# The middle group of a down projection takes its row blocks backwards, and the sums of the block at each turn stay in SBUF

## The chip, the cores and the metric

One core of one Trainium2 chip runs one layer of a streaming encoder in float32. The metric is the device time of one execution in microseconds (us). The engines are TensorE (PE, with PEld for its weight loads), VectorE (DVE), ScalarE (ACT), GpSimd (POOL) and SyncE (SP); here SP issues nearly all DMAs.

## The reference

A layer has two branches (retention and a gated linear recurrence), merged, projected and added to the residual. Behind that stands a gated MLP, and its last matrix product is the one that the change is about:

```python
h = rms_norm(x, norm2_w[l])
up = h @ ffn_w_up[l]                       # 1024 x 1024 by 1024 x 6144
gate, val = jnp.split(up, [D_FF], axis=-1)
gate = causal_depthwise_conv(gate, ffn_conv_w[l], ffn_conv_b[l])
x = x + (jax.nn.gelu(gate) * val) @ ffn_w_down[l]   # 1024 x 3072 by 3072 x 1024
return rms_norm(x, norm_f_w)
```

There are 1024 positions, D_MODEL is 1024 and D_FF 3072.

## The kernel before

**Products.** A float32 operand is split into a high part and a low part in fp32r (`split`, L595 to L600: a cast on ACT at L598, a subtraction on DVE at L599), and a product of two operands is three matmuls (`PASSES`). A job multiplies a 256 x 1024 piece by a 1024 x 1024 operand. It does so by Strassen and Winograd's scheme (`mm_fast`, L827): seven products (`PRODS`: A11, S1, S2, A12, S3, A22, S4) of 4 x 3 = 12 matmuls in place of eight, so 84 matmuls make one job. The operand of the right side comes in seven sets of four tiles (B11, T1, T2, B21, T3, T4, B22), each tile as a high and a low part, 56 buffers in all.

**The down projection.** The 3072 rows of `ffn_w_down` are three groups of 1024, `g` = 0, 1, 2; each group has an operand `dop[g]` of its own. The 1024 rows of the output are four pairs of row blocks, `t` = 0 to 3: rows 128 t to 128 t + 127 (m = 0) and 512 higher (m = 1). With two column halves `c` a job (g, t) has four output tiles [128, 512]. `djobs` (L2125) runs the groups one after the other, and t = 0, 1, 2, 3 in each. The sums over the groups live in DRAM, in `x1_d`, which holds the residual stream: a job of any group loads its four tiles (`from_x1`, L2022 to L2027, issued at L2025 by SP), adds its product (L872 and L878 in `total`, or L2035 in `emit_down`), and in groups 0 and 1 stores them (L2039, SP). In group 2 the sum goes on to the final norm (`square`, `final`), with nothing written to `x1_d`.

Within a job the tiles are emitted in this order: (m, c) = (0, 0) after A12, (1, 1) after S3, (1, 0) after A22 and (0, 1) after S4. `ask` (L624) starts the loads one or two products ahead of that, in the program's order.

**The operand's builder.** `down_op` (L1958) loads 28 tiles of `w_dn` (L1962) or of prepared sums of them in `td_d` (L1969), and splits them. After the second job of a group, `down_post` (L2116) puts the builder of the next group's operand in a list; `build` (L741) lets it go on after each product, as long as the buffer pool has room:

```python
while builders and budget > 0 and len(U) >= state["reserve"] and U.free() >= SPARE:
```

The reserve is 12 (`TIGHT`) from then on, and `SPARE` is 8. The last job of a group (`last`) gives the operand's buffers back, eight after each product, so the next operand takes the places of the old one while that is used for the last time.

**Buffers.** The pool `u` has 81 buffers of [128, 512] float32 (`NU`). `get` takes the one that was given back first, `put` gives one back. Each buffer is a place in SBUF with a name of its own, so a get makes the instructions of the new owner wait for those of the old one.

**Order.** The program is built twice. From the first build `Plan.order` (L496) works out an order of the instructions of every queue (PE, DVE, ACT, POOL, SP): the draft with the least time in its own replays, out of some 150 drafts with offsets drawn at random. The second build is tied to that order. So the place of an instruction in its queue is the planner's; what may overtake what is limited by data and by the buffers.

In the profile `x1_d` is named x_d, and a PSUM bank of `mm_fast` is g.

Of the kernel before, what the change touches and what calls it, by code (L numbers as in the profile page):

```python
# [93 lines left out]
class Units:  # L94
# [18 lines left out]
    def get(self, dt=F32):  # L113
        _, _, i = heapq.heappop(self.q)
        self.count += 1
        t = self.pool.tile(self.shape, dt, tag=f"{self.name}{i}", name=f"{self.name}{i}_{self.count}")
        self.at[id(t)] = (i, t)
        return t

    def put(self, *tiles, late=LATE):  # L120
        for t in tiles:
            self.count += 1
            heapq.heappush(self.q, (self.now[0] + late, self.count, self.at.pop(id(t))[0]))
# [430 lines left out]
def tile_trunk_layer(ctx, tc, x, xt, front, positions, params, consts, normf, w_in, w_v, w_ro, w_lo,  # L554
# [983 lines left out]
    def from_sg_t1(n):  # L1538
        def fetch(m, h):
            t = get()  # L1540
            SY.dma_start(t, t1_d[2 * n + m, :, TH * h:TH * h + TH])
            return from_sg(1, n)(m, h), t
        return fetch
# [274 lines left out]
    for n in range(4):  # L1818
        ojobs.append(Job(pair_src(w_lo, n), u, emit_lru_o(n), fast=True, last=n == 3, mate=n in (0, 2),
                         fetch=from_sg_t1(n)))  # L1820
# [15 lines left out]
    def from_x(t):  # L1836
        def fetch(m, c):
            acc = get()
            SY.dma_start(acc, x[x_row(t, m, c)])
            return acc  # L1840
        return fetch
# [78 lines left out]
    def out_start():  # L1920
# [4 lines left out]
                 pre=((0, 0), (0, 1), (1, 1)), fetch=from_x(t), mate=t == 0, prods=FIRST if t < 2 else PRODS,  # L1925
# [32 lines left out]
    def down_op(g):  # L1958
        def fetch(n, j):
            t = get()  # L1960
            kh, c = int(n[1]) - 1, int(n[2]) - 1
            SY.dma_start(t, w_dn[8 * g + 4 * kh + j, :, TH * c:TH * c + TH])  # L1962
            return t

        def either(n, j):
            if n[0] == "B":
                return fetch(n, j)
            t = get()
            SY.dma_start(t, td_d[g, int(n[1]) - 1, j])  # L1969
            return t  # L1970

        yield from operand(dop[g], either, False, ("B11", "T1", "T2", "B21", "T3", "T4", "B22"))
# [45 lines left out]
    def x1_at(t, m, c):  # L2018
        r0 = 512 * m + 128 * t
        return x1_d[r0:r0 + 128, TH * c:TH * c + TH]  # L2020

    def from_x1(t):  # L2022
        def fetch(m, c):
            acc = get()
            SY.dma_start(acc, x1_at(t, m, c))  # L2025
            return acc
        return fetch  # L2027

    def emit_down(g, t, fast):
        def emit(m, c, src, unit):  # L2030
            if fast and unit is not None:
                acc = unit
            else:
                acc = djobs[4 * g + t].take(m, c)
                V.tensor_add(acc, src, acc)  # L2035
                if unit is not None:
                    put(unit)
            if g < 2:
                ST.dma_start(x1_at(t, m, c), acc)  # L2039
                put(acc)  # L2040
                return
            fin[m, c] = acc
            square(m, c)
            if (m, 1 - c) in fin:
                final(t, m, c)
        return emit

    def square(m, c):

        o, acc = get(), fin[m, c]  # L2050
        V.tensor_mul(o, acc, nf[c])
        j = psa.get()
        S.activation(j, acc, AF.Square, scale=1.0 / 32.0, accum_out=nst[:, c, 2 + m:3 + m])
        psa.put(j)
        put(acc)
        fin[m, c] = o
        if (m, 1 - c) not in fin:
            V.tensor_scalar(nst[:, c, 2 + m:3 + m], nst[:, c, 2 + m:3 + m], EPS, None, ALU.add)
        else:
            V.tensor_add(nst[:, 2, 2 + m:3 + m], nst[:, 0, 2 + m:3 + m], nst[:, 1, 2 + m:3 + m])  # L2060
# [29 lines left out]
    def final(t, m, c):  # L2090
        v, r = (nst[:, i, 2 + m:3 + m] for i in (2, 3))
        G.tensor_tensor(r, v, half[:, 0:1], ALU.pow)
        r0 = 512 * m + 128 * t
        def scaled(c):
            o = fin.pop((m, c))
            if (m, c) == (0, 1) or t == 3:
                ins = V.tensor_scalar(o, o, r, None, ALU.mult)
            else:
                ins = S.activation(o, o, AF.Copy, scale=r)
            (SY if c else nc.scalar).dma_start(out[r0:r0 + 128, TH * c:TH * c + TH], o)  # L2100
            put(o)
            return ins

        scaled(0)
        if t == 3:
            fin["rest"] = lambda: scaled(1)
        else:
            scaled(1)

    def norm_weights():  # L2110
        for c in range(2):
            t = get()
            SY.dma_start(t, normf[:, TH * c:TH * c + TH].to_broadcast((P, TH)))
            nf.append(t)

    def down_post(g, t):  # L2116
        def fn():
            if t == 1 and g < 2:
                state["reserve"] = TIGHT
                builders.append(down_op(g + 1))  # L2120
            if g == 1 and t == 3:
                norm_weights()
        return fn

    djobs = [Job(lambda m, kh, t=t, g=g: ff_d[g, 4 * m + t, kh].rearrange("p k c -> p (k c)"), dop[g],  # L2125
                 emit_down(g, t, True), down_post(g, t), fast=True, last=t == 3,
                 prods=ENDING if (g, t) == (2, 3) else PRODS,
                 halves=(slice(0, TH // 2), slice(TH // 2, TH)) if (g, t) == (2, 3) else (),
                 pre=((0, 0), (0, 1), (1, 1)), fetch=from_x1(t),
                 ready=lambda m, kh, g=g: state["ff"] >= 8 * g + 4 * kh + 4)  # L2130
             for g in range(3) for t in range(4)]
    queue.extend(ups + djobs)
    run(wjobs)
    run(ups)
# [66 lines left out]
```

## Time and profile before

| | us |
|---|---|
| median of 3 runs | 1565.41 |
| lowest, highest | 1564.99, 1566.33 |
| the profiled execution | 1564.81 |
| its span, first to last instruction | 1563.0 |
| granted clock of TensorE, mean | 0.999 |

The profile is of one execution. Its busy times are by engine; PE's matmuls are pipelined. A group of instructions is one line, engine, operation and tile; "waits" are the idle stretches of an engine just before an instruction, put down to what ended them. A DMA's duration on SP is that of its issue; the time to landing stands apart.

### The profile page before, as it was taken

How to read it: one execution, taken by the hardware profiler on the slowest of the kernel's cores; microseconds unless marked ns; L12 is line 12 of the kernel's file. 1: busy time of each engine (PE TensorE's matmuls, PEld its weight loads, DVE VectorE, ACT ScalarE, POOL GpSimd, SP SyncE). 2: the span in 40 equal slices, each digit the busy share in tenths (PEclk: the TensorE clock that was granted, in tenths of full speed). 3: DMA queues.
4: the chain of work that ended last, by engine and by line, in shares of the span. 5: the costliest groups of instructions: out<-in, count | busy, mean ns of one | idle time of the engine just before them, and what ended most of it. 6: DMA issues, size and time to landing. Idle time of an engine off the chain costs nothing.

```text
span 1563.0 us, 21782 instructions
## 1 busy us (share of the span) xinstructions
PE 1555.2 (99%) x7081; PEld 1289.0 (82%) x7081; DVE 1356.7 (87%) x2454; ACT 971.2 (62%) x1733; POOL 64.5 (4%) x81
## 2 busy tenths in 40 slices
PE   9999999999999999999999999999999999999998
PEld 7888888888888888888888888888888888888887
DVE  8999989999999988999998898777777778887885
ACT  8557967777678787855556665545545447463653
POOL 0001001000000000000000001000000000000000
PEclk9999999999999999999999999999999999999999
DMA  9344334455354336775995246444444476787752
GB/s 325 118 144 129 122 122 137 132 186 185 103 187 142 117 126 200 257 270 168 323 309 183 94 121 222 139 138 135 140 143 140 144 235 207 243 272 249 262 189 80
DMA packets 158577, 279.04 MB, mean 179 GB/s; under 512 B 17144, under 2 KB 30848, under 8 KB 158464
## 3 DMA queue, kind: packets, MB, share of 16 engines
q1 hardware_dynamic: 152800, 261.86, 51.4%
q0 software_dynamic: 4224, 13.64, 2.7%
q10 hardware_dynamic: 1440, 2.17, 0.4%
q8 instruction: 55, 0.90, 0.2%
q14 instruction: 58, 0.48, 0.1%
HBM read 192.65 MB, written 83.89 MB: 177 GB/s over the span
## 4 chain that ended last, share of the span: by engine, by line
PE 96%; ACT 2%; DMA 1%; issue 0%; DVE 0%; POOLq 0%; POOL 0%; SPq 0%; ACTq 0%
PE g L849 85%; PE g L1616 5%; PE a L1259 3%; PE a L1387 1%; DMA u<-td_d 1%; PE a L1401 1%; PE a L1390 1%; PE a L1893 0%; PE a L1377 0%; PE a L1460 0%; ACT w L598 0%; ACT u L598 0%; PE a L1335 0%; DMA cst<-front 0%; ACT L1215 0%
## 5 line engine op out<-in xcount | busy, mean ns | idle before, releaser
L849 PE MATMUL g<-u,w 128*128 128x512 f32 x6060 | 1409.2, 390 | 0.5 <-ACT u L901 0.5
L849 PEld LDWEIGHTS g<-u,w 128*128 128x128 f32 x6060 | 1128.2, 188 | 228.9 <-ACT u L901 1.7
L598 ACT CAST w<-w 128x512 fp32r<-128x512 f32 x519 | 318.8, 621 | 317.1 <-PE g L849 233.5
L599 DVE TENSOR_TENSOR w<-w,w 128x512 fp32r<-128x512 f32 x519 | 353.1, 686 | 81.0 <-ACT w L598 78.0
L598 ACT CAST u<-u 128x512 fp32r<-128x512 f32 x245 | 146.7, 619 | 59.1 <-PE g L849 7.5
L599 DVE TENSOR_TENSOR u<-u,u 128x512 fp32r<-128x512 f32 x245 | 161.9, 686 | 6.3 <-ACT u L598 2.4
L901 ACT COPY u<-g 128x512 f32<-128x512 f32 x148 | 86.2, 582 | 60.3 <-PE g L849 57.4
L878 DVE TENSOR_TENSOR u<-g,u 128x512 f32<-128x512 f32 x146 | 100.3, 688 | 21.3 <-PE g L849 17.2
L1945 DVE SCALAR_TENSOR_TENSOR u<-u,par,u 128x511 f32<-128x511 f32 (+1 forms) x96 | 71.7, 748 | 12.8 <-ACT u L1942 12.2
L1616 PE MATMUL g<-w,u 128*128 128x512 f32 x252 | 59.0, 390 | 0.0
L1616 PEld LDWEIGHTS g<-w,u 128*128 128x128 f32 x252 | 47.1, 188 | 10.3 <-ACT g L1678 0.4
L1950 POOL DMA_DIRECT2D ff_d<-u x48 | 36.1, 753 | 447.7 <-DVE u L1949 437.3
L684 DVE TENSOR_TENSOR w<-w,w 128x512 f32<-128x512 f32 x72 | 49.4, 686 | 2.3 <-DMA w<-mix_d 1.0
L898 ACT COPY g<-g 128x512 f32<-128x512 f32 x70 | 40.5, 578 | 16.4 <-PE g L849 16.4
L1259 PE MATMUL a<-u,u 128*128 128x512 f32 x192 | 50.2, 390 | 0.1
L687 DVE TENSOR_TENSOR w<-w,w 128x512 f32<-128x512 f32 x72 | 49.4, 686 | 0.6
L693 DVE TENSOR_TENSOR w<-w,w 128x512 f32<-128x512 f32 x72 | 49.3, 685 | 0.5 <-DMA w<-mix_d 0.4
L690 DVE TENSOR_TENSOR w<-w,w 128x512 f32<-128x512 f32 x72 | 49.4, 686 | 0.2
L1942 ACT ACTIVATE u<-u,par 128x512 f32<-128x512 f32 x48 | 39.2, 817 | 8.6 <-DVE u L878 6.9
L1259 PEld LDWEIGHTS a<-u,u 128*128 128x128 f32 x192 | 35.9, 188 | 8.0 <-ACT u L598 0.5
L872 DVE TENSOR_TENSOR u<-u,u 128x512 f32<-128x512 f32 x34 | 23.2, 688 | 20.5 <-ACT u L901 20.4
L1206 ACT COPY u<-g 128x512 f32<-128x512 f32 x56 | 32.5, 581 | 8.8 <-PE g L849 8.8
(222 smaller groups left out, 1218.2 us busy)
## 6 DMA issues: line engine op xcount, KB each, us to landing
w<-w_in SPq DMA_DIRECT2D x96, 256.0 KB, 2.7
w<-w_up SPq DMA_DIRECT2D x96, 256.0 KB, 2.7
u<-w_dn SPq DMA_DIRECT2D x84, 256.0 KB, 3.2
u<-x_d SPq DMA_DIRECT2D x52, 256.0 KB, 4.8
x_d<-u SPq DMA_DIRECT2D x48, 256.0 KB, 3.4
ff_d<-u POOLq DMA_DIRECT2D x48, 256.0 KB, 3.1
td_d<-u SPq DMA_DIRECT2D x48, 256.0 KB, 3.1
u<-td_d SPq DMA_DIRECT2D x48, 256.0 KB, 4.4
```

The costliest lines, as they stand in the source:

```text
L598: S.copy(hi, src)
L599: V.tensor_sub(lo, src, hi.bitcast(F32))
L684: V.tensor_add(s, r["A21"], r["A22"])
L687: V.tensor_sub(s, s, r["A11"])
L690: V.tensor_sub(s, r["A12"], s)
L693: V.tensor_sub(src, r["A21"], r["A11"])
L849: PE.matmul(bank[:, s], w[a][:, c], need(op, (SETS[nm], j))[b][:, s], start=first and n == 0, stop=n == 11, skip_group_check=True)
L878: V.tensor_add(u, bank, u)
L901: S.copy(u, bank)
L1259: PE.matmul(ps, wg[g][a][:, cs], xs[k][b], start=q == 0, stop=q == 5)
L1616: PE.matmul(bank, o[p][:, c], w[q], start=first and j == n == 0, stop=j == 3 and n == 2, skip_group_check=True)
L1945: V.scalar_tensor_tensor(c[:, s:], src[:, :TH - s], w, c[:, s:], ALU.mult, ALU.add)
```

## The change

The list `SNAKE` gives the order of the 12 jobs: group 0 takes t = 0, 1, 2, 3, group 1 takes 3, 2, 1, 0, and group 2 again 0, 1, 2, 3. So the last job of a group and the first one of the next work on the same row blocks: (0, 3) and (1, 3), (1, 0) and (2, 0). At these two turns the four output tiles aren't stored to `x1_d`: `emit_down` puts them in a dictionary `turn`, and the next job's fetch takes them from there in place of a new buffer and a load. What depended on t = 1 or t = 3 (the start of the next operand's builder, the load of the final norm's weights, and `last`) now goes by the place in the group.

```diff
+    SNAKE = [(g, t) for g in range(3) for t in ((3, 2, 1, 0) if g == 1 else (0, 1, 2, 3))]
+    turn = {}
+
-    def from_x1(t):
+    def from_x1(g, t):
         def fetch(m, c):
+            if g and SNAKE.index((g, t)) == 4 * g:
+                return turn.pop((m, c))
             acc = get()
             SY.dma_start(acc, x1_at(t, m, c))
             return acc
...
-                acc = djobs[4 * g + t].take(m, c)
+                acc = djobs[SNAKE.index((g, t))].take(m, c)
                 V.tensor_add(acc, src, acc)
                 if unit is not None:
                     put(unit)
+            if g < 2 and SNAKE.index((g, t)) == 4 * g + 3:
+                turn[m, c] = acc
+                return
             if g < 2:
                 ST.dma_start(x1_at(t, m, c), acc)
                 put(acc)
...
     def down_post(g, t):
         def fn():
-            if t == 1 and g < 2:
+            i = SNAKE.index((g, t)) - 4 * g
+            if i == 1 and g < 2:
                 state["reserve"] = TIGHT
                 builders.append(down_op(g + 1))
-            if g == 1 and t == 3:
+            if g == 1 and i == 3:
                 norm_weights()
         return fn
...
-                 emit_down(g, t, True), down_post(g, t), fast=True, last=t == 3,
+                 emit_down(g, t, True), down_post(g, t), fast=True, last=SNAKE.index((g, t)) % 4 == 3,
...
-                 pre=((0, 0), (0, 1), (1, 1)), fetch=from_x1(t),
+                 pre=((0, 0), (0, 1), (1, 1)), fetch=from_x1(g, t),
...
-             for g in range(3) for t in range(4)]
+             for g, t in SNAKE]
```

## The prediction

> **What bounds the kernel now.** I read the page first (busy shares and the costliest groups), then the waits of the matmul engine, then its timeline over the down projection, and last its pace in stretches with much and with little DMA traffic.
>
> ```profile
> span 1563.0 us, 21782 instructions
> PE 1555.2 (99%) x7081; PEld 1289.0 (82%) x7081; DVE 1356.7 (87%) x2454; ACT 971.2 (62%) x1733; POOL 64.5 (4%) x81
> ```
>
> PE is busy for 1555.2 of 1563.0 us, so 7.8 us of the span are not PE. The waits of PE over the whole span are two rows, and the second is the whole of those in the down projection:
>
> ```profile
> PE g L1651 <- DVE st L1825: 1.0, 1, 1.0
> PE g L849 <- ACT u L901: 0.5, 2, 0.3
> ```
>
> The timeline of PE from 1320 us on, and the first entry and the end of the chain of work that ended last:
>
> ```profile
> 1319.79 79.95 PE L849 MATMUL g<-u,w 128*128 128x512 f32 x352
> 1399.98 76.45 PE L849 MATMUL g<-u,w 128*128 128x512 f32 x336 [0.24 <-ACT u L901]
> 1476.72 80.23 PE L849 MATMUL g<-u,w 128*128 128x512 f32 x364 [0.29 <-ACT u L901]
> 5.20 2.68 PE g L1668 x10
> ```
>
> The down projection is 12 jobs of 7 products of 12 matmuls, so a group of four jobs is 336 matmuls: the middle piece, 76.45 us. PE stops for 0.24 us and for 0.29 us, one group apart. From a stop on, two products of the old group are left (A22 and S4, 24 matmuls by 76.45 / 336 = 0.2275 us, 5.5 us), so the turns between the groups lie near 1405.4 and 1482.2 us. The rest of PE's idle time is the start (first matmul at 5.20 us) and the end (the last matmul ends at 1476.72 + 80.23 = 1556.95, 6.05 us before the span does). The change touches neither: its first edit is an addition in the job ahead of the first turn, and the last job keeps its rows and its place.
>
> So the most that the change can save is 0.53 us of PE's waits, unless PE's own pace depends on the transfers. That is the next thing to look at (PE's stretches, with the DMA share and GB/s at the end of the row):
>
> ```profile
> 1388.20:1407.30 19.10, 18.86 (x83) 15.29 (x83) 17.80 (x30) 14.83 (x27) 0.00 (x0) 1.00 0.97 327
> 1407.30:1426.30 19.00, 19.00 (x85) 15.73 (x85) 15.19 (x25) 7.53 (x14) 0.00 (x0) 1.00 0.98 357
> 1521.70:1540.70 19.00, 19.00 (x85) 15.73 (x84) 13.06 (x25) 9.71 (x20) 1.52 (x2) 1.00 0.21 70
> 1540.70:1563.00 22.30, 16.25 (x84) 13.74 (x82) 10.61 (x24) 7.78 (x21) 1.76 (x3) 0.95 0.26 94
> ```
>
> The first two stretches hold the first turn, with the DMA engines full; the third is quiet. PE begins 85 matmuls in 19.00 us at a DMA share of 0.98 and 85 in 19.00 us at 0.21, with the granted clock at 1.00 in both. Its pace doesn't depend on the traffic.
>
> A rule of the Trainium skill speaks against reading 99% as a bound (Perfetto Trace Analysis, Identifying the Most-Contended Engine): matmul busy time says little of the distance to the peak, since matmuls are pipelined, and weight-load busy time is the better sign. By it the 82% on PEld would leave room that fewer transfers might free; the two equal stretches, with the same PEld 15.73, say that they would not.
>
> **The change part by part.**
>
> *Transfers removed.* At each of the two turns the four sums of one row block are neither stored (L2039) nor read back (L2025): 8 stores and 8 loads of 256 KB, 16 x 0.262 = 4.2 MB.
>
> ```profile
> DMA packets 158577, 279.04 MB, mean 179 GB/s; under 512 B 17144, under 2 KB 30848, under 8 KB 158464
> L2025 SPq DMA_DIRECT2D u<-x_d x48: 319/320/1409, 1261.0 to 1527.1; - x48
> DMA to landing us min/median/max: 2.5/5.1/6.5
> L2039 SPq DMA_DIRECT2D x_d<-u x32: 319/320/396, 1339.9 to 1488.4; - x32
> DMA to landing us min/median/max: 2.0/3.6/6.4
> ```
>
> Laid end to end they would be 8 x 5.1 + 8 x 3.6 = 69.6 us, and 16 x 0.32 = 5.1 us of SP's issue time. On the path stands none of it but what lies behind the two stops. These come from a chain that the waits of the other engines show:
>
> ```profile
> ACT u L598 <- DMA u<-td_d: 2.3, 3, 1.0
> ACT u L598 <- DMA u<-w_dn: 1.4, 1, 1.4
> ACT w L598 <- DMA w<-ff_d: 3.2, 1, 3.2
> ACT u L901 <- DMA x_d<-u: 2.3, 1, 2.3
> ...
> 1393.27 5.47 DMA u<-td_d
> 1398.74 0.02 issue
> 1398.76 0.02 ACTq L598
> 1398.78 0.04 issue
> 1398.82 0.62 ACT u L598
> 1399.44 0.49 ACT u L901
> ...
> 1466.26 5.88 DMA u<-td_d
> ```
>
> The next group's operand (28 tiles) is loaded and split in the last job of the old group. One of its loads lands after 5.47 us; ACT, which takes its instructions in order, holds the cast (L598) for it, the PSUM copy behind it (L901) comes late, and PE waits for that copy. In the same 1388 to 1407 us the DMA share is 0.97. Of the 16 removed transfers, few fall into the 5.5 us before each stop (SP's queue in the timeline):
>
> ```profile
> 1392.30 0.38 SPq L2025 DMA_DIRECT2D u<-x_d  x1
> ...
> 1394.92 0.38 SPq L2025 DMA_DIRECT2D u<-x_d  x1
> ...
> 1396.99 0.40 SPq L2039 DMA_DIRECT2D x_d<-u  x1
> ```
>
> The store at 1396.99 is the first kept sum's; of the x_d loads from 1392.30 to 1394.92, three in all, the trace doesn't tell whose they are. So the loads of the operand come sooner by somewhere between nothing and 256 KB at 327 GB/s, 0.8 us, for each transfer gone. One is enough for either stop. Bounds of this term: 0 and -0.53 us. I take half, **-0.27 us**, since this trace doesn't show whether the transfers gone are ahead of the load that is late.
>
> *Buffers held.* Four [128, 512] buffers of the pool `u` (81) stay taken from the emission in one job to the addition in the next: 84 matmuls by 0.2275, 19.1 us. Before, each was put back, and taken again one or two products ahead of its use. What this can delay is the builder of the next operand, which stops when the pool has fewer than 12 free (`reserve`, L743) or fewer than 8 that were freed long enough ago (`SPARE`). Followed through the allocations of the program before: from the first kept sum to the end of that operand, the builder is called with 24 to 33 buffers in the pool, 17 to 24 of them old enough. Four fewer leave at least 20 and 13, above 12 and 8. So the builder issues the same tiles at the same products. What does change is which buffer each get receives: one freed up to four releases later. Lower bound 0. Upper bound: the releases come in eights at the end of a product, so a load that needs such a buffer waits at most one product more, 12 x 0.2275 = 2.73 us a turn, 5.5 us in all, if no slack takes it up. Value: **0**, by the row nearest to it, the loads of td_d that already come late: ACT waits 2.3 us for them and PE only 0.5.
>
> *Rows backwards.* Group 1 reads its ff_d blocks in the order 3, 2, 1, 0; as many loads of the same size (L650). The nearest store and load of one row block of x1 move from four jobs apart to three (block 2 at the first turn, block 1 at the second): 3 x 19.1 = 57 us. A load can't go out before the store has landed; 57 less the longest store and the longest load, 6.4 and 6.5, leaves 44 us in which to issue it. Cost 0; that room is the cover, and a load that came late would hold L2035 or L872 on DVE and the splits (L599) queued behind.
>
> *Additions.* All stay: the kept tile is what L2035 or L872 adds to. In the job after a turn that addition waits for one of the job before on its own engine (DVE), 19 us earlier, in place of a DMA. DVE holds nothing behind it. Cost 0.
>
> *A new plan.* `Plan.order` writes the order of every queue from a search over the whole program (150 drafts with random offsets and landing times). Sixteen DMAs fewer give it other random numbers, so order moves everywhere, in stages that the change doesn't touch too. The trace of before can't show what the new draw costs. Lower bound: PE waits 1.5 us in all, so at best -1.0 us beyond the term above, and that 1.0 is at the start, where there is little to reorder: I take the lower end as -0.3. Upper bound by the nearest rows: the four waits of ACT for DMAs quoted above, 2.3 + 1.4 + 3.2 + 2.3 = 9.2 us in one stage, all but 0.5 of it hidden now; an order that exposed a third of it would cost 3. Value **+0.3 us**, since PE's waits are near the least that they can be and a fresh draw can hardly be better; ends -0.3 and +3.
>
> **Sum.** -0.27 + 0 + 0 + 0 + 0.3 = 0.0 us. Of the profiled execution, 1564.81 us (span 1563.0 and 1.8 around it), that makes 1564.8; it stands 0.6 below the median of the three runs, 1565.41 (1564.99 to 1566.33). The forecast for the median is **1565.4 us**.
>
> **The rivals.**
>
> *The transfers were on the path (faster).* If the 69.6 us of landings were waited for, the time would be near 1496. Against it: PE waits 0.5 us in the whole stage, so no more than that can come back. Faster by more than 0.2% (3.1 us) would need six times the stage's waits. The same end by another way, a PE that runs faster beside fewer transfers, is shut out by the 85 matmuls in 19.00 us twice. Chance 1 in 100 for both. The Trainium skill's price for one DMA (DMA: Bandwidth & Descriptors, Anatomy of one DMA), about 2 us fixed and the bytes at 436 GB/s, would make 16 x 2.6 = 42 us of them, an estimate; the trace has 3.6 and 5.1 us for one, and hides them all alike.
>
> *The held buffers starve the builder (slower).* Place: the last two products before a turn and the first four after it, when 28 operand tiles must be cast and subtracted.
>
> ```profile
> L598 ACT CAST u<-u 128x512 fp32r<-128x512 f32 x245 | 146.7, 619 | 59.1 <-PE g L849 7.5
> L599 DVE TENSOR_TENSOR u<-u,u 128x512 fp32r<-128x512 f32 x245 | 161.9, 686 | 6.3 <-ACT u L598 2.4
> ```
>
> That is 28 x 0.686 = 19.2 us of DVE beside the jobs' own work; DVE is busy 17.80 of 19.10 us in the stretch before the turn, so 1.3 us are free there, and 3.8 in the one behind it. It decides where a tile is put off by more than that slack: one product (2.73 us) at each turn exceeds the 1.3, and PE would then wait up to 2.73 us twice, 1565.4 + 5.5 = 1570.9. For it: L901 waited 2.3 us for a buffer whose x_d store had not landed, so the pool is tight. Against it: the gates of the builder have room for four, and the store behind that wait is of the kind that goes. Chance 6 in 100.
>
> *An unlucky plan (slower).* Waits that are hidden now come up anywhere in the 1563 us: 3 to 8 us, 1569 to 1573. Chance 8 in 100. A milder one, 1 to 3 us, belongs to the forecast's range.
>
> *The change doesn't do what it says.* If the sums went to x1 all the same, the time would be 1565.4 with 48 loads and 32 stores. By the code the four tiles go to `turn` and come back from it before any store. 1 in 100; it ends within 0.2%.
>
> **How the numbers follow.** A difference of about 0.2%, 3.1 us, is what a measurement of this kernel can tell from none. The forecast (1564.4 to 1568.4) has 84 in 100. Its lower end is 1565.4 - 0.5 - 0.3, less some 0.2 of the runs' spread; its upper end 1565.4 + 3. With the 1 in 100 of no change in work, within 0.2% comes to 0.84: 0.85 less the 1 in 100 of the forecast that lies above 3.1. Slower: 0.06 + 0.08 + 0.01 = 0.15. Faster: 0.01. The range asked for is the forecast's own, 1564.4 to 1568.4, as it leaves out 15 in 100.
>
> **What would show it right or wrong.**
>
> ```profile
> u<-x_d SPq DMA_DIRECT2D x52, 256.0 KB, 4.8
> x_d<-u SPq DMA_DIRECT2D x48, 256.0 KB, 3.4
> ```
>
> x_d<-u should go from 48 issues to 40 and u<-x_d from 52 to 44 on the page, the traffic from 279.04 to 274.8 MB, with 7081 matmuls as before and the piece of PE between the turns at 76.2 to 76.5 us. PE's waits on L901 by the turns should lie between 0 and 1 us. DVE's and ACT's busy times stay. The forecast is wrong if PE shows waits of over 1 us at a turn (then ACT's waits for td_d or w_dn loads say whether a buffer or the traffic is behind it), or anywhere before 1260 us (then it is the plan); or if matmuls begin closer together than 0.2271 us (79.95 / 352), which would mean that the traffic did slow PE.

## The result, and the profile after

The changed kernel takes 1571.53 us (median of 5 runs, 1568.16 to 1572.57) against 1565.25 us of before in the same session: a ratio of 1.0037, 95% interval 1.0026 to 1.0048. It is slower by 6 us, where no change was forecast, and outside the range that was given. The profiled execution took 1569.5 us.

The page of after, the lines that answer to those of before (span and busy times, DMA packets, loads of x_d):

```profile
span 1567.7 us, 21756 instructions
PE 1555.3 (99%) x7081; PEld 1288.7 (82%) x7081; DVE 1355.8 (86%) x2454; ACT 972.0 (62%) x1734; POOL 67.5 (4%) x81
DMA packets 156273, 274.84 MB, mean 175 GB/s; under 512 B 16888, under 2 KB 30592, under 8 KB 156160
u<-x_d SPq DMA_DIRECT2D x44, 256.0 KB, 3.9
```

The work is what the change says: 8 loads of x_d fewer (52 to 44), 8 stores fewer (48 to 40) and 4.2 MB less traffic. Four of the engines are as busy as before to within 1 us, and PE's 1555.3 us are those of before to 0.1; POOL alone has 3.0 us more (67.5 after 64.5). So the 4.7 us that the span has grown are idle time of PE. Its waits in after, over the whole span:

```profile
PE a L1087 <- POOL rcol L1085: 2.5, 1, 2.5
PE g L1668 <- DVE u L1603: 1.1, 1, 1.1
PE g L1651 <- DVE st L1825: 1.0, 1, 1.0
PE a L1893 <- DVE u L1887: 0.8, 1, 0.8
PE g L849 <- ACT u L901: 0.6, 2, 0.3
PE g L1668 <- DVE w L599: 0.2, 1, 0.2
```

They sum to 6.2 us; before had 1.0 and 0.5. The difference of 4.7 is the span's. The turns have no more than 0.1 of it. PE's timeline over the down projection in after has the two stops it had before, of 0.31 us each in place of 0.24 and 0.29, and the same 76.46 us between them:

```profile
1404.66 76.46 PE L849 MATMUL g<-u,w 128*128 128x512 f32 x336 [0.31 <-ACT u L901]
1481.43 80.23 PE L849 MATMUL g<-u,w 128*128 128x512 f32 x364 [0.31 <-ACT u L901]
```

The loss lies at the other end of the kernel. L1668 and L1085 to L1087 belong to the first stage (the projection `w_v`, with the row norms of x beside it), some 1300 us ahead of the first turn. (The 0.8 us at L1893, near 850 us, come back as 0.7 in e1 and e9 below, whose times are those of before.) The two places in before (timeline; SP's issue of the load of `front` and the instruction that needs it, then the chain of the norms: L1084 on VectorE, a pow of 8 columns on POOL, a transpose on PE):

```profile
1.19 0.42 SPq L1645 DMA_DIRECT2D u<-front  x1
...
5.06 0.41 DVE L1603 TENSOR_SCALAR u<-u,cst 128x384 fp32r<-128x384 f32 x1
...
66.18 0.17 DVE L1084 TENSOR_SCALAR nst<-nst 128x8 f32<-128x8 f32 x1
66.25 0.69 DVE L1749 TENSOR_TENSOR u<-g,u 128x512 f32<-128x512 f32 x1
66.42 1.65 POOL L1085 TENSOR_TENSOR rcol<-nst,half 128x8 f32<-128x8 f32 x1 [65.98 <-DVE nst L1084]
66.85 0.75 DVE L1754 SCALAR_TENSOR_TENSOR u<-u,par,u 128x512 f32<-128x512 f32 x1
...
67.51 0.69 DVE L599 TENSOR_TENSOR w<-w,w 128x512 fp32r<-128x512 f32 x1
...
70.11 0.27 PE L1087 MATMUL a<-cst,rcol 128*8 128x128 f32 x1
```

And in after:

```profile
1.18 0.43 SPq L1590 DMA_DIRECT2D u<-xt  x1
...
1.66 0.42 SPq L1645 DMA_DIRECT2D u<-front  x1
...
6.39 0.42 DVE L1603 TENSOR_SCALAR u<-u,cst 128x384 fp32r<-128x384 f32 x1 [1.22 <-DMA u<-front]
...
67.65 0.16 DVE L1084 TENSOR_SCALAR nst<-nst 128x8 f32<-128x8 f32 x1
67.73 0.74 DVE L1754 SCALAR_TENSOR_TENSOR u<-u,par,u 128x512 f32<-128x512 f32 x1
67.89 6.30 POOL L1085 TENSOR_TENSOR rcol<-nst,half 128x8 f32<-128x8 f32 x1 [67.45 <-DMA v_d<-u]
68.39 0.68 DVE L599 TENSOR_TENSOR u<-u,u 128x512 fp32r<-128x512 f32 x1
...
71.40 1.28 DVE L599 TENSOR_TENSOR u<-u,u 128x512 fp32r<-128x512 f32 x2
72.61 0.68 DVE L1749 TENSOR_TENSOR u<-g,u 128x512 f32<-128x512 f32 x1
...
74.25 0.27 PE L1087 MATMUL a<-cst,rcol 128*8 128x128 f32 x1 [2.50 <-POOL rcol L1085]
```

The time from the issue of the load of `front` to its landing (last figure of the row), in before and then in after:

```profile
u<-front SPq DMA_DIRECT2D x1, 256.0 KB, 3.1
```
```profile
u<-front SPq DMA_DIRECT2D x1, 256.0 KB, 4.7
```

The load of `front` is third in SP's queue where it was second. It is issued 0.47 us later, takes 1.6 us longer to land, and PE stands 1.1 us at L1668 for it. The pow, the same instruction on the same 128 x 8 numbers, takes 6.30 us where it took 1.65. What differs beside it is VectorE's order: in before an addition that reads PSUM (L1749) runs as the pow begins; in after L1754 and seven of L599 run first, all with two tiles from SBUF as sources, and the pow ends 1.58 us after the next PSUM read begins (67.89 + 6.30 - 72.61). (The store of v_d that the row names as the pow's releaser isn't what held it: L1084, whose result it needs, ended at 67.81.) In both places the order of a queue differs, and the order of all queues is the planner's.

### The profile page after: what moved, and what is told of

Read it like the earlier page. It is cut to its first block, busy times and chain, and to the rows that moved or that the text cites. A ratio compares the mean times of both kernels' runs of the same rounds, so it can differ in the third digit from the quotient of the medians.

```text
span 1567.7 us, 21756 instructions
## 1 busy us (share of the span) xinstructions
PE 1555.3 (99%) x7081; PEld 1288.7 (82%) x7081; DVE 1355.8 (86%) x2454; ACT 972.0 (62%) x1734; POOL 67.5 (4%) x81
## 2 busy tenths in 40 slices
DMA packets 156273, 274.84 MB, mean 175 GB/s; under 512 B 16888, under 2 KB 30592, under 8 KB 156160
## 4 chain that ended last, share of the span: by engine, by line
PE 93%; DMA 2%; DVE 2%; ACT 2%; issue 1%; POOL 0%; SPq 0%; POOLq 0%; ACTq 0%; DVEq 0%
PE g L849 82%; PE g L1616 4%; PE a L1259 3%; DMA u<-td_d 1%; PE a L1387 1%; PE a L1401 1%; DMA u<-x 1%; PE a L1390 1%; PE a L1893 0%; PE a L1377 0%; PE a L1460 0%; DVE w L599 0%; POOL rcol L1085 0%; DMA w<-mix_d 0%; DMA u<-front 0%
## 5 line engine op out<-in xcount | busy, mean ns | idle before, releaser
L849 PE MATMUL g<-u,w 128*128 128x512 f32 x6060 | 1408.9, 390 | 0.6 <-ACT u L901 0.6
L849 PEld LDWEIGHTS g<-u,w 128*128 128x128 f32 x6060 | 1128.1, 188 | 229.0 <-ACT u L901 1.5
L599 DVE TENSOR_TENSOR w<-w,w 128x512 fp32r<-128x512 f32 x519 | 352.5, 684 | 88.6 <-ACT w L598 82.8
L599 DVE TENSOR_TENSOR u<-u,u 128x512 fp32r<-128x512 f32 x245 | 161.9, 681 | 4.3 <-DMA u<-sg_d 2.1
L901 ACT COPY u<-g 128x512 f32<-128x512 f32 x148 | 86.1, 582 | 64.3 <-PE g L849 62.9
L872 DVE TENSOR_TENSOR u<-u,u 128x512 f32<-128x512 f32 x34 | 23.2, 687 | 19.5 <-ACT u L901 19.4
L1949 DVE TENSOR_TENSOR u<-u,u 128x512 f32<-128x512 f32 x48 | 32.9, 687 | 5.5 <-ACT u L1948 5.4
```

Source lines behind the costliest of these rows:

```text
L599: V.tensor_sub(lo, src, hi.bitcast(F32))
L849: PE.matmul(bank[:, s], w[a][:, c], need(op, (SETS[nm], j))[b][:, s], start=first and n == 0, stop=n == 11, skip_group_check=True)
L901: S.copy(u, bank)
```

## The experiments

The theory, **order**: the planner drew another order for the whole program, and what was lost is lost where that order is worse, not where the kernel was changed. The rival, **change**: fewer transfers or buffers held longer cost the time by themselves. For the long pow the theory is **port**: POOL doesn't get at SBUF while VectorE runs instructions with two SBUF sources back to back. Its rival is **slow pow**: the operation itself takes 6.3 us there, whatever stands beside it. Each kernel is the one of before or after with the order of its queues set or drawn anew; no line of the computation differs. In e1 to e9 the line numbers near the start are two higher than in before (L1087 is the pow, L1089 the transpose, L1605 the old L1603, L1670 the old L1668, L1751 the PSUM addition, L601 and L851 are L599 and L849); e10 to e12 have those of after. In the code `...` stands for lines that aren't shown. Medians of after and of an experiment come from different sessions, so each ratio is to before of the experiment's own session.

**e1, the change in the old order.** The program of before is built and planned, its order is carried over instruction by instruction, and the 16 transfers are dropped from it (`gone` holds them).

```diff
-    draft, steps = build()
-    nc, _ = build(Plan(steps, draft).order())
+    draft, old = build(snake=False)
+    gone = set(MARK["gone"])
...
+    was = Plan(old, draft)
+    draft, new = build()
+    now = Plan(new, draft)
+    left = [s for s in old if s.name not in gone]
+    to = same(left, new)
+    order = {e: [to[n] for n in q if n in to and n not in gone and to[n] in now.steps] for e, q in was.order().items()}
...
+    nc, _ = build(order)
```

> The program is that of after (16 transfers fewer, four sums kept at each turn, same SBUF places), but every queue runs in the order that the plan of before gave it, with the 16 transfers taken out. Theory 'order' (the time went because the search drew another order, and two thirds of the new waits are in the first 75 us): PE waits back to 1.5 to 2.0 us in all, the product L1668 and the transpose L1087 without a wait on L1603 or L1085, time 1565.3 within 1 us. Rival 'change' (fewer transfers or held buffers cost the time, whatever the order): 1571.5 as after. If the turns gain what the prediction took for them, 0.3 to 0.5 us below before; the waits on L901 by the turns say so.

1565.01 us against 1565.41, ratio 0.9998 (0.9989 to 1.0007). PE's waits in e1, all of them, and its timeline from 1299.70 us to the end of the matmuls:

```profile
PE g L1653 <- DVE st L1827: 1.0, 1, 1.0
PE a L1895 <- DVE u L1889: 0.7, 1, 0.7
```
```profile
1299.70 258.02 PE L851 MATMUL g<-u,w 128*128 128x512 f32 x1148
```

The change alone costs nothing that can be measured, to within the 1.1 us of the interval's upper end. Nor does it show a gain: PE runs through both turns in one piece of 258.02 us, but so it does in e5 below, which is the program of before in its own order there. The stops of some 0.3 us come and go from one execution to the next: the same file of after has both in its first profile, one in e10, none in e11 and e12.

**e2 and e3, the first 110 us alone.** The head of every queue (475 instructions of PE's) is taken from the other kernel's order: after with the head of before, and before with the head of after.

```diff
...
+    order = {e: [to[n] for n in old_o[e] if n not in gone][:cut[e]] + new_o[e][cut[e]:] for e in old_o}   # e2
+    order = {e: [back[n] for n in new_o[e][:cut[e]]] + old_o[e][cut[e]:] for e in old_o}                  # e3
```

> The program of after with its own order, except for the head of every queue (475 of PE's 7049 instructions, some 110 us), which has the order of before. Theory 'order': the waits of the first 75 us go (1.1 + 0.2 at L1668 and 2.5 at L1087, 3.8 in the profiled execution of after, more in its slower runs), those behind stay (0.8 at L1893, 0.6 on L901): 1566 to 1567. Rival 'change': 1571.5, since the first 110 us hold none of the change.

> The program of before, nothing changed in it, with its own order except for the same head of every queue, which has the order of after. Theory 'order': 3.8 us or more are added without any change to the down projection: 1569 to 1571.5, with PE waiting for L1603 and L1085. Rival 'change': 1565.3.

e2: 1565.72 us, ratio 1.0002 (0.9993 to 1.0010). e3: 1570.36 us, ratio 1.0032 (1.0019 to 1.0044). PE's waits in e2, all of them, and the two longest in e3, a program in which nothing of the down projection is changed:

```profile
PE g L1653 <- DVE st L1827: 1.0, 1, 1.0
PE a L1895 <- DVE u L1889: 0.7, 1, 0.7
PE g L1618 <- ACT u L1601: 0.4, 1, 0.4
PE g L851 <- ACT w L600: 0.2, 1, 0.2
```
```profile
PE a L1089 <- POOL rcol L1087: 2.5, 1, 2.5
PE g L1670 <- DVE u L1605: 1.6, 1, 1.6
```

So the slowdown goes with the first 110 us of the order, to and fro, and has nothing to do with whether the sums stay in SBUF. e2 came 0.3 us below its range of 1566 to 1567: the waits on L901 that were to stay are not in its profile.

**e4 and e5, the pow.** One VectorE instruction is moved: in after's order the next PSUM addition up, to stand right behind L1084; in before's order the one that stands there seven places down.

```diff
...
+    q = order["DVE"]
+    at = q.index(MARK["mean"])
+    n = next(n for n in q[at:] if n in MARK["bank"])   # e4
+    q.remove(n)
+    q.insert(at + 1, n)
...
+    n = q.pop(at + 1)                                  # e5
+    q.insert(at + 8, n)
```

> The program and the order of after, with one VectorE instruction moved: the next addition of a PSUM bank (L1749) runs straight behind L1084, before the run of L599. In after the pow on POOL (L1085) took 6.30 us from 67.89, and ended 1.6 us after the first VectorE instruction that reads PSUM (72.61); all those between read two SBUF tiles. In before it began beside such an addition and took 1.65 us. Theory 'port': POOL gets no SBUF access while VectorE runs instructions with two SBUF sources back to back; the pow takes 1.6 to 2 us, PE's 2.5 us on L1087 go, time 2.5 us or more below after. The Trainium skill's page SBUF - State Buffer, Two separate sides, states such a lock. Rival 'slow pow' (its first use, or a fetch): 6.3 us and the wait stay, 1571.5.

> The program and the order of before, with one VectorE instruction moved the other way: the PSUM addition (L1749) behind L1084 goes seven instructions later, behind L1754 and six of L599, which all read two SBUF tiles. Theory 'port': the pow starts as before, near 66.4, but ends 1.6 us after the first PSUM read, which begins near 70.5: 5.7 us in place of 1.65, PE waits some 2.0 us at the transpose, 1567.4. Rival 'slow pow': 1.65 us and no wait, 1565.4.

e4: 1567.07 us, ratio 1.0013 (1.0004 to 1.0022), 4.5 us below after's median. The wait that is gone was 2.5; what makes up the other 2.0 stands in no profile (see e10 to e12). e5: 1567.37 us, ratio 1.0017 (1.0009 to 1.0026), 2.3 above the 1565.08 of before by one instruction moved. POOL's timeline in e4, then POOL and VectorE in e5:

```profile
68.40 1.65 POOL L1087 TENSOR_TENSOR rcol<-nst,half 128x8 f32<-128x8 f32 x1 [67.95 <-DMA v_d<-u]
```
```profile
66.77 5.69 POOL L1087 TENSOR_TENSOR rcol<-nst,half 128x8 f32<-128x8 f32 x1 [66.32 <-DVE nst L1086]
```
```profile
70.87 1.28 DVE L1751 TENSOR_TENSOR u<-g,u 128x512 f32<-128x512 f32 x2
```

In e5 the pow ends at 72.46, 1.59 us after that PSUM read begins. 'Slow pow' falls: the place of one VectorE instruction makes the pow 1.65 or 5.7 us long. 'Port' forecast both lengths; that such a row of instructions always keeps POOL out is refuted by e7, e8 and e10 (last section).

**e9, both places mended.** As e4, and in SP's queue the load of `front` one place up.

```diff
+    q = order["SP"]
...
+    q.remove(MARK["front"])
+    q.insert(1, MARK["front"])
```

> The program and the order of after with two instructions moved: the PSUM addition behind L1084 as in e4, and on SP the load of front (L1645) one place ahead, second in its queue as in before, where after has a load of xt ahead of it. Theory 'order': these two places are the whole loss; the wait at L1668 for L1603 (1.6 in e4) goes as well, PE waits 1.8 us or less in all, 1565.4 within 0.7. If something else in the changed program costs time: e4's 1567.1 less 1.6 isn't reached.

1565.76 us, ratio 1.0005 (0.9996 to 1.0014), without a wait at L1668 or at the transpose; one of its twelve executions, without a profile, took 5613.42 us. Two instructions out of place account for the slowdown, as far as the interval tells (up to 2.2 us could remain). The wait at L1668 that e4 still has, then PE's waits in e9, all of them:

```profile
PE g L1670 <- DVE u L1605: 1.6, 1, 1.6
```
```profile
PE g L1653 <- DVE st L1827: 1.0, 1, 1.0
PE a L1895 <- DVE u L1889: 0.7, 1, 0.7
PE g L851 <- ACT w L600: 0.4, 1, 0.4
```

They sum to 2.1 us, above the 1.8 that was expected.

**e6, e7 and e8, other draws.** The planner's random numbers start elsewhere, in before (e6 from 2, e7 from 3) and in after (e8 from 2).

```diff
-        r = np.random.RandomState(1)
+        r = np.random.RandomState(2)
```

> The program of before, with the planner's random numbers started from 2 in place of 1. Theory 'order': nothing of the work changes and the time moves all the same, somewhere from 1565 to 1572, with the new waits of PE anywhere; off from 1565.4 by over 1.5 us in at least one of the two draws of before (random numbers from 2 and from 3). Rival 'change': 1565.4 within 1 us for both.

> The program of before, with the planner's random numbers started from 3. As for the draw from 2: theory 'order' from 1565 to 1572, rival 'change' 1565.4 within 1 us.

> The program of after, with the planner's random numbers started from 2. Theory 'order': another draw, from 1565 to 1572, and no nearer to 1571.5 than to 1565.4 by rule; the waits of PE at L1603 and at the pow need not come again. Rival 'change': 1571 within 1 us, since the change is still there.

Before drawn anew takes 1569.49 us (ratio 1.0029, 1.0019 to 1.0039) and 1566.42 (1.0005, 0.9996 to 1.0014); after drawn anew 1565.35 (1.0002, 0.9993 to 1.0011). One of three is off by 4 us with no change in the work, and the changed kernel with another draw is as fast as before. In e6's profiled execution (1567.42 us) the loss is the pow again:

```profile
PE a L1089 <- POOL rcol L1087: 3.0, 1, 3.0
```

**e10, e11 and e12, the changed kernel again.** The same file, for more profiles: e5's profile had shown a dip of PE's clock behind its wait. e5's stretches (PE busy first, then PEld, DVE, ACT and POOL; the granted clock third from the end):

```profile
72.00:76.00 4.00, 3.48 (x10) 2.76 (x11) 4.00 (x8) 0.25 (x1) 0.46 (x1) 0.60 0.84 283
76.00:80.00 4.00, 4.00 (x19) 3.29 (x18) 1.89 (x4) 0.00 (x0) 0.00 (x0) 0.97 0.92 240
```

> The changed kernel once more, for a second profile: half of its executions took 1571.5 or more, while the profiled one took 1569.5, with PE's granted clock at 1.00 all through. In e5 the clock fell to 0.60 from 72 to 76 us behind a wait of 1.9 us, and PE was busy 1.4 us longer. Theory 'clock': a wait of 2 to 3 us at the transpose is followed in part of the executions by such a dip, worth 1.5 to 2.5 us; an execution of 1571 or more shows it, one of 1568 to 1570 doesn't. Rival: the slower executions have longer waits, at 1.00.

> The changed kernel a third time, for one more profile; as for the second: theory 'clock', an execution of 1571 or more has a dip of the granted clock behind the wait at the transpose; rival, it has longer waits at a clock of 1.00.

> The changed kernel a fourth time, for one more profile. Theory 'clock': if it takes 1571 or more, the granted clock dips behind a wait of PE, as in e5; if it takes 1568 to 1570 it has the waits alone. Rival: 1571 or more with longer waits at a clock of 1.00. One execution can fall on the fast side and settle nothing.

e10 took 1571.69 us in the median of four runs (ratio 1.0046, 1.0032 to 1.0060), but its profiled execution 1568.33; e11 1568.44 and e12 1569.90, one run each. All three profiled executions fell below 1571, so what the executions of 1571 to 1574 do was not seen. Their mean granted clock is on record. In e5 the four executions of 1568.21 us and more have 0.998, the seven shorter ones 0.999 or 1.000. In e10 the two longest, 1572.09 and 1573.97, have 0.997, the profiled one 0.999; 0.002 of 1567 us are 3.1 us. But 1571.30 in e10 and 1572.09 among the first five runs of after have 0.999 as well. That speaks for the clock as a part of it and doesn't settle it.

Two things came out beside. In e10 the pow took 2.08 us, in the same order in which it took 6.30 and 6.29 in after, e11 and e12, so the order makes the long pow likely, not certain. And e12's PE was busy 1557.2 us, 2 us more than in before, and the place was another than expected: behind its wait at L1668 (timelines of PE in e12, then in e11)

```profile
6.38 4.02 PE L1668 MATMUL g<-w,u 128*128 128x512 f32 x9 [0.39 <-DVE u L1603]
```
```profile
7.11 2.33 PE L1668 MATMUL g<-w,u 128*128 128x512 f32 x9 [1.39 <-DVE u L1603]
```

nine matmuls took 4.02 us there against 2.33, at a granted clock of 1.00 in both. The wait isn't shown to be the cause: behind longer waits (1.14 us in after, 1.65 in e3) the nine took 2.32 and 2.35 us, and in e1, without that wait, the twelve matmuls of L1670 took 4.24 us against 3.61 in e9.

## Why the prediction was wrong

The forecast, 1565.4 us between 1564.4 and 1568.4, missed by one term of its sum: the new plan, taken at +0.3 us, cost some 6. The signs of the work all came (44 loads, 40 stores, 274.84 MB, 76.46 us between the turns). So did the sign that was named for the plan: waits of PE of over 1 us ahead of 1260 us, 2.5 and 1.1.

**The bound** held. PE is the bound, its pace didn't move with the traffic (76.45 and 76.46 us for the 336 matmuls between the stops), and the waits that the turns could give back were 0.5 us. One reading was off, without weight for the sum: PE's first matmul begins at 0.99 us (behind the wait on L1825), not at 5.20, which is the chain's first entry for PE.

**Transfers removed**, taken at -0.27 us between 0 and -0.53: not shown. After's profiled execution has both stops (0.62 us in all, 0.09 more than before), e1 has none, and e5, with all 48 loads of x_d still in it, has none either. So e1 can't say that the transfers were behind them. The 42 us that the prediction works out from the Trainium skill carry no term; the section that it names (DMA: Bandwidth & Descriptors, Anatomy of one DMA) fits DMAs issued by GpSimd, and SP issued these.

**Buffers held**, taken at 0: right, as far as e1 can tell. In e1 the four buffers are held in the order of before, and PE doesn't wait at the turns. The rival of a starved builder forecast 1570.9, near what was measured, by a mechanism that did not happen.

**Rows backwards** and **additions**, 0: right by e1, whose whole ratio is 0.9998 (at most 1.0007).

**A new plan**, taken at +0.3 between -0.3 and +3: this is the step that failed. That the order would move everywhere was in the text; its size was not. The upper end was made from waits of ACT for DMAs in the down projection, the stage of the change, while the new order is drawn for all stages, and I set the first stage aside as one "where there is little to reorder". It is where the loss came: 1.1 to 1.6 us at L1668 and 2.5 at the transpose, and on top of them what the slower executions add, whose cause stays open. The rows of before would have told that these places are thin. The load of `front`, issued at 1.19, landed 3.1 us later, near 4.3, and L1603 ran at 5.06: some 0.8 us to spare, where the landing in after came 2.1 us later (1.66 + 4.7). The pow feeds a transpose that the later matmuls stand behind, 2.0 us after the pow's end (70.11 - 68.07); the long pow took 4.65 us more. What the rows of before couldn't tell is that a pow of 1.65 us may take 6.30. A better bound would have come from drawing anew: e6 to e8 span 1565.35 to 1569.49, and after is one more draw at 1571.5.

**The chances** followed from that. The unlucky plan had 8 in 100, and the time that it named, 1569 to 1573, was the measured one, by the mechanism that it named, waits anywhere in the program. In hindsight, with three of five draws (before, e8, and e7 with its 1566.4) within 0.2% and two not, it should have had some 3 or 4 in 10, and the range should have reached to 1573.

## What to carry to other kernels

Where a search orders a whole program, a small change is a new draw: compare it at the same order, by carrying the order over, before anything is said of the change. The spread of the draws was some 6 us here, and the most that the change could gain 0.5. A tiny operation on POOL that a busy PE waits for is safer beside a VectorE instruction that reads PSUM than ahead of a row of VectorE instructions with two SBUF sources: 1.65 us each time there, 2 to 7 us here.

## What the runs showed of the hardware

The pow on POOL took 1.65 us in before, e1, e2, e4 and e9, where a PSUM addition on VectorE ran as it began. In the other nine profiles it began 0.16 to 0.18 us into a VectorE instruction with two SBUF sources, with more of them behind. In six of these (after, e3, e5, e6, e11 and e12) it took 5.69 to 6.90 us and ended 1.58 to 1.60 us after the first PSUM read began. In the other three (e7, e8 and e10) it took 2.02 to 2.08 us with no PSUM read in time, and ended 1.58 or 1.59 us after the next VectorE instruction began, itself one with two SBUF sources. The rows of e10, in the order of after:

```profile
68.10 0.74 DVE L1754 SCALAR_TENSOR_TENSOR u<-u,par,u 128x512 f32<-128x512 f32 x1
68.76 0.68 DVE L599 TENSOR_TENSOR u<-u,u 128x512 fp32r<-128x512 f32 x1
```
```profile
68.26 2.08 POOL L1085 TENSOR_TENSOR rcol<-nst,half 128x8 f32<-128x8 f32 x1 [67.81 <-DMA v_d<-u]
```

So in all nine the pow looks held until one VectorE instruction begins, and takes 1.6 us from there. At the first change from one two-source instruction to the next it got in three times of nine; in the other six it was held up to the PSUM read, past seven to nine such instructions. What decides that is open.

The Trainium skill (SBUF — State Buffer, SBUF: two separate sides) states that VectorE instructions with two SBUF sources and POOL instructions that read SBUF share ports by an exclusive lock, held for a whole instruction. On POOL's side the runs agree, and add that a row of such instructions back to back can keep POOL out for 4 us and more. On VectorE's side no wait shows: in before L1754 and L599 ran 0.75 and 0.69 us, their usual lengths, from 66.85 and 67.51, while the pow is listed from 66.42 to 68.07. So, if POOL's row is right, not all of its 1.65 us can have held the lock against VectorE.

PE's granted clock fell to 0.60, the mean of 4 us, behind a wait of 1.92 us in e5, and not behind waits of 2.5 us in after and 3.0 us in e6. The Trainium skill (TensorE: Matmul & The Clock Gate, HAM oscillation) puts the gap that throttles at over some 3.4 us; e5's was shorter. So a wait of 2 us can have a second price, seen in one of the six profiles with a long pow: PE was busy 1556.6 us in e5 against 1555.2.
